# Loading and folding the Fourier input weights before the last modulation chunks

## The chip, the cores and the metric

The kernel runs on one core of a Trainium2 chip. The metric is the device time of one execution in microseconds (us), as the median of several runs. The core has five engines with instruction streams of their own: PE (TensorE, matrix multiply, with weight loads shown apart as PEld), DVE (VectorE), ACT (ScalarE), POOL (GpSimd) and SP (SyncE, which here only issues transfers). Sixteen DMA engines move the data. Each engine carries out its instructions in the order in which they were put into its queue.

## The reference

One encoder layer is applied to two sequences of 1024 tokens with 1024 channels, each with a conditioning vector `c`.

```python
mod = silu(c) @ w_ada + b_ada                  # 6 x 1024: shift, scale, gate, twice
h = rmsnorm(x, g_mix) * (1.0 + sc1) + sh1
z = h @ w_in                                   # q latent 256, kv latent 128, rotary key 64, Fourier 512
y_mla = mla_group(z[:, :256], z[:, 256:384], z[:, 384:448], ...)   # latent attention, 4 heads
y_four = fourier_group(z[:, 448:], w_four)     # real part of a 2-D FFT over tokens and 64 channels, 8 groups
x = x + ga1 * (concat([y_mla, y_four]) @ w_out)
h2 = rmsnorm(x, g_ffn) * (1.0 + sc2) + sh2
x = x + ga2 * ((silu(h2 @ w_gate) * (h2 @ w_up)) @ w_down)         # inner width 2816
y = rmsnorm(x, g_final)
```

All is float32. The change touches only how the weights of the Fourier part of `w_in` are made ready.

## The kernel before

Matrix products are made from two parts of each operand: `split` (lines 59 to 61) rounds a tile to a high part on ACT and takes the rest as a low part on DVE, and `mm3` (lines 70 to 73) multiplies high by high, high by low and low by high, so that lines 71, 72 and 73 carry nearly all matmuls. PSUM has eight banks, which are handed out in turn; a bank is free again when its readers are done.

The first stage reads `x` in eight pairs of 128-token blocks, four pairs for each sequence. A pair goes through these steps. `norm` (line 348) loads two blocks of `x`, squares them on ACT (L356), forms the reciprocal root on POOL (`rstd`, L95 to L102) and scales on DVE (L360). `flip` (line 363), four times per pair, transposes two of the eight channel chunks on PE (L374), applies the modulation on ACT (L377, tile `hf`) and splits the result into `hh` and `hl`. `zproj` (line 395), once for each block, multiplies by the 448 columns of the latents, `wz_h` and `wz_l`, then takes norms and the rotary key (L404 to L417), which gives `lat`. `latents` (line 425) transposes that (L431). `evenodd` (line 381) forms sum and difference of the pair's two blocks on POOL (L390) and splits them into `eoh` and `eol`, for which there are the buffers `eoh0`, `eol0`, `eoh1`, `eol1`. `fourier_in` (line 438) multiplies them by the Fourier input weights `wcs_h` and `wcs_l`. The function `pair` (line 507) sets these steps in order, with a step of `extras` (further weights, among them the folds of L242 and the second half of the modulation) between them.

Before the first pair stand the weights. `fold_q`, `fold_out` and `fold_pe` fold gains and small matrices into larger ones. The modulation vector is made from eight chunks of `w_ada`, 1 MB each: `mod_load` issues a chunk's transfer on SP, `mod_mm` (L207) multiplies it when it has landed, and after the last of them `mod_vecs` (L138 to L148) turns the row into the scales and shifts that every flip needs. The chunks share a few buffers (two `wada` buffers, and `hh0`, `hh1`, `hl1`, `hf`, which the pairs use later), so a load often has to wait until a chunk has been multiplied. `wz_load` and `wz_split` bring in the 448 latent columns in two halves, of four chunks each. `prep_wcs(i, wf)` (lines 330 to 346) folds the Fourier weights: for chunk `i` four matmuls of a slice of `wf` by the small matrix `c2` into one bank, then three casts on ACT (L337 twice, L342) and three subtractions on DVE (L338 twice, L343). Over the eight chunks these are 32 matmuls, which the profile counts as 64, 24 casts and 24 subtractions.

In the kernel before, `c2` and the Fourier weights `wfT` (two loads into the `wada` buffers, lines 489 to 493) are issued after the last modulation chunk, and the eight `prep_wcs` (lines 500 and 501) come after the flips of pair 0 and the norm of pair 1, ahead of its first `zproj`.

The order in each engine's queue is not simply that of the code. A planner walks the instructions with its own estimate of their costs: among those that it holds ready, the one that the code has first goes first, and ready work from later in the code can be put into a time in which it believes an engine idle. An instruction can be held back by hand: `behind()` (line 63) makes everything in its block go behind the last `split` on the engine concerned, ACT or DVE. It holds back no transfer and nothing on PE or POOL.

Of the kernel before, what the change touches and what calls it, by code (L numbers as in the profile page):

```python
# [12 lines left out]
F32 = mybir.dt.float32  # L13
# [8 lines left out]
P = 128  # L22
# [28 lines left out]
def hybrid_encoder_kernel(ctx: ExitStack, tc: tile.TileContext, a: dict):  # L51
    nc = tc.nc
# [3 lines left out]
    def rd(t):  # L56
        return t.bitcast(F32)

    def split(hi, lo, src):
        here["a"] = nc.scalar.copy(hi, src).ins  # L60
        here["v"] = nc.vector.tensor_tensor(out=lo, in0=src, in1=rd(hi), op=ALU.subtract).ins  # L61

    def behind():

        st = ExitStack()
        st.enter_context(tc.issue_after(here["a"]))
        st.enter_context(tc.issue_after(here["v"]))
        return st
# [63 lines left out]
    def rows(j, u):  # L132
        return slice(512 * u + P * j, 512 * u + P * j + P)
# [22 lines left out]
    with ExitStack() as st:  # L156
        p1b = st.enter_context(ExitStack())
        w2 = p1b.enter_context(tc.tile_pool(name="p1b", bufs=1, side="right", reuse_waits="tile"))
        w = st.enter_context(tc.tile_pool(name="p1", bufs=1, reuse_waits="tile"))
        pp = st.enter_context(tc.tile_pool(name="p1_ps", bufs=8, space=PSUM, reuse_waits="tile"))  # L160

        def bank():
            return pp.tile([P, 512], F32, tag="b", name="bank")

        def xtile():
            return w2.tile([P, D], F32, tag="x", name="xt", bufs=4)

        def stile(name):
            return w.tile([P, 512], F32, tag="sk", name=name, bufs=3)
# [9 lines left out]
        c2 = w.tile([P, P], F32, name="c2")  # L179
# [12 lines left out]
        def wada_tile():  # L192
            return w2.tile([P, 4, 512], F32, tag="wada", name="wada", bufs=2)

        def mod_load(c, cols, wt):
            for j, (lo_, n) in enumerate(cols):
                nj = n // 512
                nc.sync.dma_start(
                    wt[:, j * nj : (j + 1) * nj, :],
                    a["w_ada"][c * P : (c + 1) * P, lo_ : lo_ + n].rearrange("p (j n) -> p j n", n=512))  # L200
            return wt

        def mod_mm(key, c, wt):
            if c == 0:
                mods[key] = bank()
            for j in range(4):
                nc.tensor.matmul(  # L207
                    mods[key][32 * j : 32 * j + 32, :], scT[:, c, :], wt[:, j, :], start=(c == 0), stop=(c == NC - 1))

        def mod_row(key):  # L210
            mr = stile("modrow")
            nc.vector.tensor_copy(mr, mods.pop(key))
            return mr
# [24 lines left out]
        def fold_out(h, wo2, wuvT, gq):  # L238
            for g in range(2):
                gs = slice(512 * g, 512 * g + 512)  # L240
                ps = bank()
                nc.tensor.matmul(ps, wuvT[:, h, :], wo2[:, h % 2, gs], start=True, stop=True)  # L242
                so = stile("so")
                nc.vector.tensor_scalar(out=so, in0=ps, scalar1=gq[:, 2:3], scalar2=None, op0=ALU.mult)
                (nc.gpsimd if h < 2 else nc.sync).dma_start(wo_d[:, h, gs], so)
# [75 lines left out]
        def wz_load(i, t):  # L321
            t = t[:, : 4 * DZ].rearrange("p (a b) -> p a b", a=4)
            nc.sync.dma_start(t, a["wz"][:, i : i + 4, :])
            return t

        def wz_split(i, t):
            for b in range(0, 4, 2):
                split(wz_h[:, i + b : i + b + 2, :], wz_l[:, i + b : i + b + 2, :], t[:, b : b + 2, :])

        def prep_wcs(i, wf):  # L330
            ps = bank().rearrange("p (a b) -> p a b", a=4)
            for p in range(4):
                nc.tensor.matmul(ps[:, p, :], wf[:, p, (i % 4) * P : (i % 4 + 1) * P], c2, start=True, stop=True)
            for v, sl in ((ps[:, :, 0:64], slice(0, NCOS)), (ps[:, :, 64:128], slice(NZC, NCS))):
                h = wcs_h[:, i, sl].rearrange("p (a b) -> p a b", a=4)
                l = wcs_l[:, i, sl].rearrange("p (a b) -> p a b", a=4)
                nc.scalar.copy(h, v)  # L337
                nc.vector.tensor_tensor(out=l, in0=v, in1=rd(h), op=ALU.subtract)  # L338
            v = ps[:, :, 64:128:32].unsqueeze(1).broadcast_to([P, 3, 4, 2])
            h = wcs_h[:, i, NCOS:NZC].rearrange("p (k a b) -> p k a b", k=3, a=4)  # L340
            l = wcs_l[:, i, NCOS:NZC].rearrange("p (k a b) -> p k a b", k=3, a=4)
            nc.scalar.copy(h, v)  # L342
            nc.vector.tensor_tensor(out=l, in0=v, in1=rd(h), op=ALU.subtract)  # L343
# [4 lines left out]
        def norm(k):  # L348
            s, j = pairs[k]
            ms = tiny.tile([P, 2], F32, name="ms")  # L350
            xt = []
            for u in range(2):
                t = xtile()
                nc.sync.dma_start(t, xs[s][rows(j, u), :])
                jk = w.tile([P, D], BF16, tag="junk", name="junk", bufs=1)
                nc.scalar.activation(jk, t, AF.Square, scale=1.0 / 32.0, accum_out=ms[:, u : u + 1])  # L356
                xt.append(t)
            r = rstd(ms, 2)
            for u in range(2):
                nc.vector.tensor_scalar(out=xt[u], in0=xt[u], scalar1=r[:, u : u + 1], scalar2=None, op0=ALU.mult)  # L360
            st1["x", k] = xt

        def flip(k, g):
            s, j = pairs[k]
            if g == 0:
                st1["hf", k] = w2.tile([P, NC, 2, P], F32, tag="hf", name="hf", bufs=1)
                st1["hh", k] = w.tile([P, NC, 2, P], F32R, tag=f"hh{k % 2}", name="hh")
                st1["hl", k] = w.tile([P, NC, 2, P], F32R, tag=f"hl{k % 2}", name="hl")
            hf, xt = st1["hf", k], st1["x", k]
            pt = bank().rearrange("p (c u t) -> p c u t", c=2, u=2)  # L370
            for c in range(2):
                for u in range(2):
                    cc = 2 * g + c
                    nc.tensor.transpose(pt[:, c, u, :], xt[u][:, cc * P : (cc + 1) * P], ident)  # L374
            for c in range(2):
                cc = 2 * g + c
                nc.scalar.activation(hf[:, cc], pt[:, c], AF.Identity, bias=sh1[s][:, cc : cc + 1], scale=s1[s][:, cc : cc + 1])  # L377
            gs = slice(2 * g, 2 * g + 2)
            split(st1["hh", k][:, gs], st1["hl", k][:, gs], hf[:, gs])
# [74 lines left out]
        def wide(tag, shape=(P, 4, 512)):  # L454
            return (w2 if tag == "hf" else w).tile(list(shape), F32, tag=tag, name="wide")
# [12 lines left out]
        mod_mm(0, 0, wt[0])  # L468
        mod_mm(0, 1, wt[1])
        wt = [mod_load(2, cols0, wide("hh1")), mod_load(3, cols0, wada_tile())]  # L470
        fold_out(0, wo2, wuvT, gq)
        fold_out(1, wo2, wuvT, gq)
        fold_pe(wpe, gq)
        mod_mm(0, 2, wt[0])
        mod_mm(0, 3, wt[1])
        wt = [mod_load(4, cols0, wada_tile()), mod_load(5, cols0, wide("hh1"))]
        nc.sync.dma_start(bT, a["bT"])
        nc.sync.dma_start(gT, a["gT"])
# [2 lines left out]
        mod_mm(0, 4, wt[0])  # L481
        mod_mm(0, 5, wt[1])
        wt = [mod_load(6, cols0, wide("hh0")), mod_load(7, cols0, wada_tile())]
        wz_split(0, wz0)
        wz1 = wz_load(4, wide("hl1", (P, 4 * 512)))
        mod_mm(0, 6, wt[0])
        mod_mm(0, 7, wt[1])
        mod_vecs(mod_row(0), bank, bT, gT, 0, 0, s1, sh1)
        nc.sync.dma_start(c2, a["c2"])
        wf = []  # L490
        for q in range(2):
            wf.append(wada_tile())
            nc.sync.dma_start(wf[q], a["wfT"][:, :, 512 * q : 512 * q + 512])
        for g in range(4):
            flip(0, g)
        wz_split(4, wz1)
        norm(1)
        nc.sync.dma_start(ropec, a["ropec"])
        nc.sync.dma_start(ropes, a["ropes"])
        for i in range(8):  # L500
            prep_wcs(i, wf[i // 4])
        zproj(0, 0)
        evenodd(0)
        nk = len(pairs)
# [93 lines left out]
    with ExitStack() as st:  # L598
        early = st.enter_context(ExitStack())
        wa = early.enter_context(tc.tile_pool(name="p2a", bufs=1, reuse_waits="tile"))  # L600
        w = st.enter_context(tc.tile_pool(name="p2", bufs=1, side="right", reuse_waits="tile"))
# [235 lines left out]
    with ExitStack() as st:  # L837
        w = st.enter_context(tc.tile_pool(name="p3", bufs=1, side="right", reuse_waits="tile"))
# [144 lines left out]
        for k in range(nit + 4):  # L983
            if k >= nit:
                i = k - nit
# [3 lines left out]
            if k < nit:  # L989
# [3 lines left out]
                i = k % 8  # L993
# [21 lines left out]
    with ExitStack() as st:  # L1015
        w = st.enter_context(tc.tile_pool(name="p5", bufs=1, reuse_waits="tile"))
# [579 lines left out]
```

## Time and profile before

| | |
|---|---|
| median of three runs | 2137.72 us (lowest 2137.21) |
| profiled execution | 2136.0 us, span 2134.2 us |
| mean granted PE clock | 0.989 |
| busy: PE, DVE, ACT, POOL | 2054.9, 1420.7, 904.3, 826.7 us |
| moved by DMA | 371.11 MB, mean 174 GB/s |

The span is the time from the first to the last instruction that the profile shows. Busy time says how long an engine had something in work; PEclk is the share of its full clock that PE was granted. A row of a view in order of time gives the start, the duration, the engine, the line and operation, the tile written and the tiles read, the shape, the count, and in brackets the idle time of the engine ahead of it with what ended it.

### The profile page before, as it was taken

How to read it: one execution, taken by the hardware profiler on the slowest of the kernel's cores; microseconds unless marked ns; L12 is line 12 of the kernel's file. 1: busy time of each engine (PE TensorE's matmuls, PEld its weight loads, DVE VectorE, ACT ScalarE, POOL GpSimd, SP SyncE). 2: the span in 40 equal slices, each digit the busy share in tenths (PEclk: the TensorE clock that was granted, in tenths of full speed). 3: DMA queues.
4: the chain of work that ended last, by engine and by line, in shares of the span. 5: the costliest groups of instructions: out<-in, count | busy, mean ns of one | idle time of the engine just before them, and what ended most of it. 6: DMA issues, size and time to landing. Idle time of an engine off the chain costs nothing. (4 is left out here: it accounts for less than half of the span.)

```text
span 2134.2 us, 28930 instructions
## 1 busy us (share of the span) xinstructions
PE 2054.9 (96%) x10096; PEld 1671.4 (78%) x10096; DVE 1420.7 (67%) x2118; ACT 904.3 (42%) x1758; POOL 826.7 (39%) x1014
## 2 busy tenths in 40 slices
PE   5899998999999998999999999999999999999998
PEld 3787865888888886888888888887788888888876
DVE  2656655766676668786677667777866566557675
ACT  2655522555564546333333336444333333336441
POOL 1455202111222313797797720135545445420142
PEclk8999999999999999999999999999999999999999
DMA  9586656433545355564455468675423222248662
GB/s 366 189 248 181 225 189 234 102 92 92 138 119 124 119 182 203 187 212 168 159 206 188 153 227 290 226 237 175 148 79 119 99 101 97 99 135 290 230 226 101
DMA packets 184387, 371.11 MB, mean 174 GB/s; under 512 B 19280, under 2 KB 58832, under 8 KB 181168
## 3 DMA queue, kind: packets, MB, share of 16 engines
q1 hardware_dynamic: 166384, 313.80, 44.3%
q0 software_dynamic: 17856, 55.45, 8.8%
q8 instruction: 79, 1.29, 0.2%
q14 instruction: 68, 0.56, 0.1%
HBM read 257.18 MB, written 120.39 MB: 177 GB/s over the span
## 5 line engine op out<-in xcount | busy, mean ns | idle before, releaser
L71 PE MATMUL bank<-H,wh 128*128 128x512 f32 x1232 | 489.4, 397 | 13.5 <-DVE val L130 5.0
L73 PE MATMUL bank<-H,wl 128*128 128x512 f32 x1232 | 488.1, 396 | 1.5 <-DVE wl L61 1.5
L72 PE MATMUL bank<-H,wh 128*128 128x512 f32 x1232 | 488.2, 396 | 0.0
L130 DVE TENSOR_TENSOR val<-bank,val 128x512 f32<-128x512 f32 x244 | 167.0, 689 | 191.2 <-PE bank L73 183.4
L71 PEld LDWEIGHTS bank<-H,wh 128*128 128x128 f32 x1232 | 232.2, 188 | 73.2 <-DVE val L130 7.3
L73 PEld LDWEIGHTS bank<-H,wl 128*128 128x128 f32 x1232 | 232.0, 188 | 58.5 <-DVE wl L61 2.3
L72 PEld LDWEIGHTS bank<-H,wh 128*128 128x128 f32 x1232 | 232.0, 188 | 55.8
L61 DVE TENSOR_TENSOR wl<-draw,wh 128x512 fp32r<-128x512 f32 x286 | 200.9, 737 | 80.9 <-ACT wh L60 79.8
L60 ACT CAST wh<-draw 128x512 fp32r<-128x512 f32 x286 | 169.3, 619 | 155.3 <-PE bank L72 76.9
L72 PE MATMUL bank<-wl,wh 128*128 128x512 f32 x572 | 223.7, 391 | 2.2 <-DVE wl L61 2.2
L130 POOL TENSOR_TENSOR val<-val 128x512 f32<-128x512 f32 x58 | 82.8, 1434 | 363.5 <-DVE val L1380 188.6
L73 PE MATMUL bank<-wh,wl 128*128 128x512 f32 x572 | 222.6, 389 | 0.0
L71 PE MATMUL bank<-wh 128*128 128x512 f32 x572 | 222.6, 389 | 0.0
L60 ACT CAST wh<-rgu 128x512 fp32r<-128x512 f32 x172 | 106.7, 621 | 269.4 <-PE bank L72 211.5
L60 ACT CAST wh<-val 128x512 fp32r<-128x512 f32 x133 | 82.2, 621 | 277.6 <-PE bank L72 249.4
L61 DVE TENSOR_TENSOR wl<-val,wh 128x512 fp32r<-128x512 f32 x133 | 139.3, 1049 | 83.5 <-ACT wh L60 83.5
L61 DVE TENSOR_TENSOR wl<-rgu,wh 128x512 fp32r<-128x512 f32 x172 | 167.1, 972 | 4.8 <-ACT wh L60 4.2
L127 POOL TENSOR_TENSOR val<-rgu 128x512 f32<-128x512 f32 x84 | 122.0, 1452 | 120.3 <-DMA rgu<-in_wgu_dram 92.5
L72 PEld LDWEIGHTS bank<-wl,wh 128*128 128x128 f32 x572 | 107.3, 188 | 27.7 <-DVE wl L61 5.7
L71 PEld LDWEIGHTS bank<-wh 128*128 128x128 f32 x572 | 107.4, 188 | 22.3
L73 PEld LDWEIGHTS bank<-wh,wl 128*128 128x128 f32 x572 | 107.4, 188 | 22.1
L127 POOL TENSOR_TENSOR val<-val 128x512 f32<-128x512 f32 x89 | 119.4, 1358 | 1.3
(319 smaller groups left out, 4096.7 us busy)
## 6 DMA issues: line engine op xcount, KB each, us to landing
rgu<-in_wgu_dram SPq DMA_DIRECT2D x86, 512.0 KB, 4.2
draw<-s_d SPq DMA_DIRECT2D x143, 256.0 KB, 4.1
s_d<-val POOLq DMA_DIRECT2D x88, 256.0 KB, 4.1
draw<-t_d SPq DMA_DIRECT2D x88, 256.0 KB, 4.3
s_d<-val SPq DMA_DIRECT2D x66, 256.0 KB, 2.7
draw<-in_w_down_dram SPq DMA_DIRECT2D x55, 256.0 KB, 4.0
wada<-in_w_ada_dram SPq DMA_DIRECT2D x13, 1024.0 KB, 8.8
xt<-in_x_dram SPq DMA_DIRECT2D x16, 512.0 KB, 6.3
```

Source lines behind the costliest of these rows:

```text
L60: here["a"] = nc.scalar.copy(hi, src).ins
L61: here["v"] = nc.vector.tensor_tensor(out=lo, in0=src, in1=rd(hi), op=ALU.subtract).ins
L71: nc.tensor.matmul(out, lh, rh, start=first, stop=False, skip_group_check=cont)
L72: nc.tensor.matmul(out, lh, rl, start=False, stop=False, skip_group_check=cont)
L73: nc.tensor.matmul(out, ll, rh, start=False, stop=last, skip_group_check=cont)
L127: eng.tensor_tensor(out=out, in0=x, in1=y, op=ALU.subtract)
L130: eng.tensor_tensor(out=out, in0=x, in1=y, op=ALU.add)
```

## The change

The Fourier weights get four buffers of their own in place of two `wada` buffers: the bytes that `evenodd` later uses for the even and odd halves. Their loads and that of `c2` are issued behind chunk 3 of the modulation, ahead of chunks 4 to 7. The fold is done in two groups of four, one behind the multiplication of chunk 3, the other behind that of chunk 5. The second half of `wz` is loaded right behind chunk 7 as before, but its code stands ahead of the second group. Behind the modulation vectors, the split of the second half of `wz` is held behind the second flip's split, and the norm of pair 1 behind the fourth flip's.

```diff
         def prep_wcs(i, wf):
...
-                nc.tensor.matmul(ps[:, p, :], wf[:, p, (i % 4) * P : (i % 4 + 1) * P], c2, start=True, stop=True)
+                nc.tensor.matmul(ps[:, p, :], wf[:, p, (i % 2) * P : (i % 2 + 1) * P], c2, start=True, stop=True)
...
         wt = [mod_load(2, cols0, wide("hh1")), mod_load(3, cols0, wada_tile())]
+        nc.sync.dma_start(c2, a["c2"])
+        wf = []
+        for q in range(4):
+            wf.append(w.tile([P, 4, 256], F32, tag=("eoh0", "eol0", "eoh1", "eol1")[q], name="wf", bufs=1))
+            nc.sync.dma_start(wf[q], a["wfT"][:, :, 256 * q : 256 * q + 256])
         fold_out(0, wo2, wuvT, gq)
         fold_out(1, wo2, wuvT, gq)
         fold_pe(wpe, gq)
         mod_mm(0, 2, wt[0])
         mod_mm(0, 3, wt[1])
+        for i in range(4):
+            prep_wcs(i, wf[i // 2])
         wt = [mod_load(4, cols0, wada_tile()), mod_load(5, cols0, wide("hh1"))]
...
         mod_mm(0, 4, wt[0])
         mod_mm(0, 5, wt[1])
         wt = [mod_load(6, cols0, wide("hh0")), mod_load(7, cols0, wada_tile())]
+        wz1 = wz_load(4, wide("hl1", (P, 4 * 512)))
+        for i in range(4, 8):
+            prep_wcs(i, wf[i // 2])
+        wf.clear()
         wz_split(0, wz0)
-        wz1 = wz_load(4, wide("hl1", (P, 4 * 512)))
         mod_mm(0, 6, wt[0])
         mod_mm(0, 7, wt[1])
         mod_vecs(mod_row(0), bank, bT, gT, 0, 0, s1, sh1)
-        nc.sync.dma_start(c2, a["c2"])
-        wf = []
-        for q in range(2):
-            wf.append(wada_tile())
-            nc.sync.dma_start(wf[q], a["wfT"][:, :, 512 * q : 512 * q + 512])
-        for g in range(4):
-            flip(0, g)
-        wz_split(4, wz1)
-        norm(1)
+        flip(0, 0)
+        flip(0, 1)
+        with behind():
+            wz_split(4, wz1)
+        flip(0, 2)
+        flip(0, 3)
+        with behind():
+            norm(1)
         nc.sync.dma_start(ropec, a["ropec"])
         nc.sync.dma_start(ropes, a["ropes"])
-        for i in range(8):
-            prep_wcs(i, wf[i // 4])
         zproj(0, 0)
         evenodd(0)
```

## The prediction

> **What bounds the kernel now.** I read the engine totals first, then the stages of the span, because the edit lies wholly in the first fiftieth of it. In the stage table the columns after the window are its length, then busy time and count of PE, its weight loads, DVE, ACT and POOL, then PE's granted clock, the DMA share and GB/s.
>
> ```profile
> span 2134.2 us, 28930 instructions
> PE 2054.9 (96%) x10096; PEld 1671.4 (78%) x10096; DVE 1420.7 (67%) x2118; ACT 904.3 (42%) x1758; POOL 826.7 (39%) x1014
> ...
> 0.00:44.00 44.00, 22.39 (x88) 7.59 (x88) 10.33 (x21) 5.67 (x9) 6.47 (x20) 0.81 0.94 367
> 44.00:62.40 18.40, 16.08 (x109) 15.46 (x110) 12.84 (x37) 15.23 (x39) 4.35 (x8) 0.90 0.97 346
> 62.40:85.00 22.60, 18.31 (x102) 14.89 (x101) 17.32 (x48) 14.46 (x39) 10.87 (x20) 0.92 0.43 138
> 85.00:300.00 215.00, 210.50 (x1237) 164.69 (x1235) 130.56 (x262) 109.16 (x267) 80.47 (x174) 1.00 0.73 225
> 300.00:500.00 200.00, 189.05 (x1089) 155.60 (x1089) 135.91 (x275) 92.04 (x186) 32.02 (x48) 0.97 0.45 127
> 1100.00:1400.00 300.00, 300.00 (x1304) 244.39 (x1303) 207.55 (x264) 126.02 (x222) 129.49 (x119) 1.00 0.63 212
> ```
>
> PE is busy for 96% of the span and idle for 79.3 us. Of that, 21.6 us (44 - 22.39) lie in the first 44 us, 2.3 in the next stage and 4.3 in the third: 28 us is all that an edit of the start can reach. Later stages run with PE nearly full, 1100 to 1400 entirely so. Such a stage starts and ends earlier together with what precedes it, so a microsecond won before 85 us should arrive at the end, and one lost too.
>
> The first 44 us belong to the DMA. Two windows of that stage show it; below them are rows in order of time (start, duration, engine, line, what; in brackets the idle time before it and its releaser).
>
> ```profile
> 20.00:30.00 10.00, 4.96 (x29) 1.28 (x27) 2.25 (x3) 0.00 (x0) 2.30 (x5) 0.86 1.01 407
> 30.00:40.00 10.00, 2.76 (x12) 0.40 (x16) 2.05 (x3) 4.07 (x6) 1.74 (x6) 0.50 1.03 419
> ...
> 31.38 1.93 PE L207 MATMUL bank<-wide,scT 128*32 128x512 f32 x8 [5.34 <-DMA wide<-in_w_ada_dram]
> 39.18 1.94 PE L207 MATMUL bank<-wide,scT 128*32 128x512 f32 x8 [5.87 <-DMA wide<-in_w_ada_dram]
> 41.67 1.93 PE L207 MATMUL bank<-wada,scT 128*32 128x512 f32 x8 [0.56 <-DMA wada<-in_w_ada_dram]
> 44.51 1.09 PE L138 MATMUL bank<-ident,modrow 128*128 128x128 f32 x4 [0.91 <-DVE modrow L212]
> 45.39 3.01 PE L374 MATMUL bank<-ident,xt 128*128 128x128 f32 x16
> 48.24 7.31 PE L333 MATMUL bank<-c,wada 128*128 128x128 f32 x64
> 57.36 0.44 PE L71 MATMUL bank<-wz_h,hh 128*128 128x448 f32 x1 [1.81 <-DVE wcs_l L343]
> 62.39 1.03 PE L374 MATMUL bank<-ident,xt 128*128 128x128 f32 x8
> ```
>
> The 16 DMA engines are full (share 1.01 and 1.03) from 20 to 40 us, and the modulation chunks 5, 6 and 7 are multiplied when they land (31.4, 39.2, 41.7). From the end of chunk 7, at 43.60, the path is PE's own: transposes, the Fourier fold (L333, 7.31 us), 1.81 us for a bank that the fold's split still holds, and the first projection, 5.03 us, to 62.39.
>
> **The change part by part.**
>
> *Bytes moved ahead: +5.0 us.*
>
> ```profile
> wada<-in_wfT_dram SPq DMA_DIRECT2D x2, 1024.0 KB
> ```
>
> The Fourier weights, 2 x 1024 KB = 2.10 MB, were issued behind chunk 7, into its kind of buffer. Now they are ahead of chunk 4. At 419 GB/s they take 5.0 us, the DMA engines have nothing idle to put them in, so chunks 5 to 7 land 5.0 us later, chunk 7 near 46.7. Below, 4.5 is possible (the row at 407 GB/s leaves a little room); above, 5.9, if the second half of the fold, 32 matmuls, overruns the gap between chunks 5 and 6 at half clock. The four destinations are bytes that nothing has used yet, so SP has no new buffer to wait for; SP issues five loads where it issued three, at a place where DMA has megabytes queued, so the two more cost nothing there. SP's later issues, the second half of wz and x of pair 1, no longer stand behind a wait for chunk 7's buffer; the bytes before them are the same, so I count nothing for them either. POOL's queue is not passed.
>
> *The fold leaves the path: -9.1 us.* The 7.31 us of L333 and the 1.81 us behind them now lie in gaps where PE waits for chunks: the first half ahead of chunk 4, whose gap grows by the 5.0 us of new bytes, the second between chunks 5 and 6, where PE stood 5.87 us in the rows above. If that cover failed, the fold would cost its 7.31 again. Its splits go along:
>
> ```profile
> L337 ACT CAST wcs_h<-bank 128x256 fp32r<-128x256 f32 x16 | 5.3, 413 | 0.4 <-DVE wcs_l L338 0.3
> L338 DVE TENSOR_TENSOR wcs_l<-bank,wcs_h 128x256 fp32r<-128x256 f32 x16 | 6.1, 416 | 0.1
> L343 DVE TENSOR_TENSOR wcs_l<-bank,wcs_h 128x24 fp32r<-128x24 f32 x8 | 1.3, 176 | 0.2 <-ACT wcs_h L342 0.2
> ```
>
> About 7.4 us of DVE and somewhat less of ACT go where these were busy 10.33 and 5.67 us out of 44, so they are hidden.
>
> *Clock: -1.4 us.* PE's granted clock was 0.50 from 30 to 40, after long idle. With fold matmuls between the chunks PE should rest for no more than about a microsecond ahead of chunk 7, less than the 1.81 us behind which the projection still started at full speed.
>
> ```profile
> 22.85 1.04 PE L207 MATMUL bank<-wada,scT 128*32 128x512 f32 x8
> 68.13 0.60 PE L431 MATMUL bank<-ident,lat 128*128 128x128 f32 x4
> 69.44 1.88 PE L242 MATMUL bank<-wada,wuvT 128*128 128x512 f32 x4
> ```
>
> Chunk 7 then takes 1.04 in place of 1.93, and the four modulation transposes 0.60 in place of 1.09: -1.4. Bounds: nothing, and -2.3 when the flips' transposes gain as well.
>
> *The first projection is now paced by the flips: +2.8 us.* It used to find its input ready. Rows of ACT:
>
> ```profile
> 46.54 1.48 ACT L377 ACTIVATE hf<-bank,sh,s 128x256 f32<-128x256 f32 x3 [1.69 <-PE bank L374]
> 51.71 0.97 ACT L60 CAST wz_h<-wide 128x896 fp32r<-128x896 f32 x1
> 52.54 0.66 ACT L60 CAST hh<-hf 128x512 fp32r<-128x512 f32 x1
> 54.12 0.68 DVE L61 TENSOR_TENSOR hl<-hf,hh 128x512 fp32r<-128x512 f32 x1
> ```
>
> Four flips and one wz cast took 46.54 to 53.20; the other wz cast, once done ahead of them, is now behind flip 1 too: +0.9, so 54.1; the last low half adds 0.7: 54.8. Two of eight chunks are then left, six matmuls at 5.03/24 = 0.21: 56.1 on the old clock. Unpaced it would have been 62.39 - 9.1 = 53.3, hence +2.8. The bound below is 0, if the planner fills these gaps with the pair's second projection. The first projection so ends near 56.1 + 5.0 - 1.4 = 59.7.
>
> *Two stalls behind it: -5.0 us.*
>
> ```profile
> 66.88 0.68 DVE L61 TENSOR_TENSOR eol<-eo,eoh 128x512 fp32r<-128x512 f32 x1
> 72.58 0.40 PE L71 MATMUL bank<-wcs_h,eoh 128*128 128x280 f32 x1 [1.26 <-ACT hf L377]
> 78.34 0.48 DVE L416 TENSOR_SCALAR lat<-bank,rs_r 128x256 f32<-128x256 f32 x1 [1.67 <-POOL rs_r L102]
> 78.97 1.08 PE L431 MATMUL bank<-ident,lat 128*128 128x128 f32 x4 [3.03 <-DVE lat L416]
> 79.85 2.84 PE L242 MATMUL bank<-wada,wuvT 128*128 128x512 f32 x4
> 78.00:80.00 2.00, 1.03 (x5) 1.06 (x6) 1.66 (x5) 0.89 (x3) 0.77 (x4) 0.59 0.02 4
> ```
>
> DVE reached the even/odd halves' low parts only at 66.88, behind the fold's. POOL's second half, ACT's casts, and behind them the latent chain (ACT, POOL, DVE) were late in turn, and PE stood 1.26 + 3.03 us; the clock then fell to 0.59, and L431 and L242 took 1.4 us more than at full speed (1.08 - 0.60 and 2.84 - 1.88). Together 5.7. With the fold's 7.4 us gone from DVE I take 5.0; the rest is the idle per pair of the following stage, (215 - 210.5)/7 = 0.6, since the other seven pairs lie in it. Bounds: 0 and -5.7.
>
> *Pair 1's norm is put behind flip 3: +1.5 us.*
>
> ```profile
> 54.12 1.14 ACT L356 ACTIVATE junk<-xt 128x1024 bf16<-128x1024 f32 x1
> 57.01 0.23 POOL L95 TENSOR_SCALAR rs_v<-ms 128x2 f32<-128x2 f32 x1 [3.77 <-ACT wcs_h L342]
> 59.18 1.42 DVE L360 TENSOR_SCALAR xt<-xt,rs_r 128x1024 f32<-128x1024 f32 x2 [1.38 <-POOL rs_r L102]
> 72.24 0.48 DVE L259 TENSOR_TENSOR lw<-w 64x128 f32<-64x128 f32 x2
> ```
>
> From the last cast of flip 3 (54.1 + 5.0 - 1.4 = 57.7) two squares take 2.3, POOL's chain 2.2, DVE's scaling 1.4: 63.6. Pair 1's flips would ask PE for it at 59.7, and everything queued on PE behind them, the second projection first, would wait: 3.8 us, and 1.4 more if the clock falls. Against it: the planner moves ready work ahead, as it did with L259, which the code has several pairs later, and the second projection is 5 us of such work. Between 0 and 5.2 I take 1.5, by the 1.26 us that PE waited for a flip at 72.58.
>
> *The sum:* 5.0 - 9.1 - 1.4 + 2.8 - 5.0 + 1.5 = -6.2 us. The profiled execution took 2136.0 us, 1.8 outside its span; it becomes 2129.8. The median of the runs shown, 2137.72, lies 1.7 above it, so I forecast 2131.5. The planner orders the rest of the kernel anew; the idle 11 us of 300 to 500 show what an order can cost, and I allow 4 us either way.
>
> A rule that speaks against the edit: the Trainium skill, "TensorE: Matmul & The Clock Gate", Part 1 and Part 4, says that about 3.4 us of sustained work release the clock, and that transposes do not count as such work. By that rule the fold was the warm-up of the projection.
>
> ```profile
> 46.00:48.00 2.00, 2.00 (x13) 2.00 (x12) 1.80 (x10) 1.46 (x4) 0.00 (x0) 0.59 1.05 388
> ```
>
> Here the trace differs: only transposes ran from 44.51 to 48.13, and within this window the clock left 0.50.
>
> **The rivals.**
>
> *The projection starts cold.* The first 3 us of it run at half clock: 8 of 16 matmuls are done, 8 x 0.21 = +1.6, and the -1.4 is lost: 2134.5. For it: 27 to 47 us was at half clock. Against: the row just shown.
>
> *The latent chain still ends last.* The stalls at 72.58 and 78.97 stay, since POOL and ACT are in them as well as DVE: 5.0 - 9.1 - 1.4 + 2.8 + 1.5 = -1.2, so 2136.5. For it: 78.34 names POOL. Against: POOL was idle before, and stood behind late ACT work.
>
> *Slower: pair 1 arrives late.* The planner keeps the flips ahead of the second projection, PE waits 3.8 and pays 1.4 of clock, and as the chain hangs on the same engines the old stalls stay: 5.0 - 9.1 + 2.8 + 5.2 = +3.9, so 2141.6. It decides once this wait exceeds the stalls won by 1.3 us.
>
> *Everything is filled.* The second projection covers pacing and norm: 5.0 - 1.4 - 9.1 - 5.7 = -11.2, so 2126.5.
>
> *The change does not do what it says.* The planner leaves L333 behind chunk 7, or the loads behind the chunks: the path is that of before, 2137.7.
>
> **How the numbers follow.** Forecast 0.47, latent chain 0.20, slower 0.12, filled 0.10, cold 0.06, nothing done 0.05. With the 4 us of the planner around the outer cases the range is 2123 to 2142. Every case is within 2%, which is 43 us and about what a measurement of this kernel can tell from no change; I leave 0.02 and 0.03 for effects of the new order that no row here shows.
>
> **What would show it.** L333 in two groups before chunk 6, idle-free of DMA; chunk 7's L207 near 46.7 and shorter than 1.9; the first L71 at 448 columns near 53 with gaps, its group over by 60; no wait above 1 us at L431; L360 of pair 1 near 62 to 64. I would be wrong if chunk 7 came later than 48, if PE stood for L374 of pair 1, or if the idle time after 85 us changed by more than 4 us.

## The result and the profile after

The changed kernel takes 2142.09 us (median of 22 runs) against 2138.98 us for the kernel before beside it: a ratio of 1.0017, 95% interval 1.0012 to 1.0023. That is 3.1 us more by the medians, 3.6 by the ratio, well within the 2% and still clear of no change. The forecast was 2131.5, a gain of 6.2 us on the 2137.72 of before. The profiled execution took 2141.93 us.

The engine totals and the stage table of the changed kernel, columns as in the prediction:

```profile
span 2140.2 us, 28935 instructions
PE 2056.4 (96%) x10096; PEld 1674.6 (78%) x10096; DVE 1420.1 (66%) x2118; ACT 904.0 (42%) x1758; POOL 825.8 (39%) x1014
...
0.00:44.00 44.00, 25.39 (x136) 16.11 (x136) 13.61 (x40) 10.81 (x31) 6.08 (x18) 0.91 0.93 359
44.00:62.40 18.40, 11.71 (x58) 6.28 (x59) 12.21 (x25) 11.05 (x21) 3.05 (x4) 0.85 0.96 384
62.40:85.00 22.60, 16.39 (x85) 13.68 (x83) 13.19 (x37) 13.06 (x34) 13.04 (x28) 0.85 0.26 79
85.00:300.00 215.00, 210.34 (x1245) 165.89 (x1245) 129.66 (x262) 109.16 (x267) 79.72 (x173) 1.00 0.73 225
1100.00:1400.00 300.00, 300.00 (x1304) 244.81 (x1303) 206.85 (x261) 124.52 (x220) 129.78 (x120) 1.00 0.63 212
```

The fold is out of PE's path: the first stage holds 48 more of PE's instructions than before, the second 51 fewer. But the third, which should have become fuller, has 2 us less of PE work in it than before, at a mean clock of 0.85. PE's instructions in order of time show where:

```profile
26.83 10.01 PE L333 MATMUL bank<-c,wf 128*128 128x128 f32 x64 [2.60 <-DMA wf<-in_wfT_dram]
38.44 1.07 PE L207 MATMUL bank<-wide,scT 128*32 128x512 f32 x8 [0.60 <-DMA wide<-in_w_ada_dram]
45.79 1.93 PE L207 MATMUL bank<-wide,scT 128*32 128x512 f32 x8 [6.28 <-DMA wide<-in_w_ada_dram]
48.28 1.60 PE L207 MATMUL bank<-wada,scT 128*32 128x512 f32 x8 [0.56 <-DMA wada<-in_w_ada_dram]
50.80 0.63 PE L138 MATMUL bank<-ident,modrow 128*128 128x128 f32 x4 [0.92 <-DVE modrow L212]
51.26 1.91 PE L374 MATMUL bank<-ident,xt 128*128 128x128 f32 x16
54.45 0.47 PE L71 MATMUL bank<-wz_h,hh 128*128 128x448 f32 x1 [1.27 <-ACT hh L60]
58.98 0.47 PE L71 MATMUL bank<-wz_h,hh 128*128 128x448 f32 x1 [1.04 <-ACT hh L60]
62.73 0.36 PE L73 MATMUL bank<-wz_h,hl 128*128 128x448 f32 x1
69.30 0.66 PE L374 MATMUL bank<-ident,xt 128*128 128x128 f32 x2 [6.21 <-DVE xt L360]
76.96 0.60 PE L431 MATMUL bank<-ident,lat 128*128 128x128 f32 x4
```

The first four rows are the fold and chunks 5, 6 and 7; chunk 4 follows the fold at 36.77. The planner put all eight folds into one group ahead of chunk 4, and they run while the chunks arrive. Chunk 7 starts at 48.28 (41.67 before). The first projection is paced by the flips, as the prediction said, and ends at 63.09 (62.39 before). Then PE stands 6.21 us for pair 1's scaled `x`. No such wait was there before. And its clock (the third number from the right) falls:

```profile
64.00:66.00 2.00, 0.00 (x0) 0.00 (x0) 0.28 (x2) 0.88 (x2) 1.84 (x4) 1.00 0.01 4
66.00:68.00 2.00, 0.00 (x0) 0.00 (x0) 0.00 (x0) 0.36 (x1) 1.76 (x6) 0.62 0.00 0
68.00:70.00 2.00, 0.70 (x3) 0.73 (x4) 1.60 (x4) 0.00 (x0) 1.70 (x7) 0.50 0.00 0
70.00:72.00 2.00, 2.00 (x9) 1.76 (x9) 1.24 (x3) 0.24 (x1) 0.59 (x2) 0.50 0.04 8
```

What came between the flip and its input is in the rows of ACT, POOL and DVE, in the order of the chain:

```profile
60.28 1.10 ACT L356 ACTIVATE junk<-xt 128x1024 bf16<-128x1024 f32 x1
61.84 1.09 ACT L356 ACTIVATE junk<-xt 128x1024 bf16<-128x1024 f32 x1
62.78 1.27 POOL L390 TENSOR_TENSOR eo<-hf 128x512 f32<-128x512 f32 x1 [1.98 <-DVE eol L61]
64.14 0.23 POOL L95 TENSOR_SCALAR rs_v<-ms 128x2 f32<-128x2 f32 x1
64.45 1.26 POOL L390 TENSOR_TENSOR eo<-hf 128x512 f32<-128x512 f32 x1
65.67 0.72 POOL L98 TENSOR_TENSOR rs_y<-rs_v,mhalf 128x2 f32<-128x2 f32 x1
66.74 0.22 POOL L95 TENSOR_SCALAR rs_v<-mz 128x2 f32<-128x2 f32 x1
68.17 0.20 POOL L102 TENSOR_TENSOR rs_r<-rs_w,rs_y 128x2 f32<-128x2 f32 x1
68.40 1.42 DVE L360 TENSOR_SCALAR xt<-xt,rs_r 128x1024 f32<-128x1024 f32 x2 [4.12 <-POOL rs_r L102]
```

The squares, held behind flip 3, the last of the four, begin at 60.28. POOL is then busy with pair 0's sums and differences (L390), and mixes the first projection's root (`mz`) into pair 1's, which takes from 64.14 to 68.37; before it took 2.1 us (57.01 to 59.15).

A good mark for the end of the disturbed part is the copy of pair 0's second Fourier product, L446 writing `zs`, before and after:

```profile
85.57 0.37 ACT L446 COPY zs<-bank 128x256 f32<-128x256 f32 x1 [0.42 <-PE bank L73]
```

```profile
88.29 0.37 ACT L446 COPY zs<-bank 128x256 f32<-128x256 f32 x1 [2.23 <-PE bank L73]
```

2.7 us later at this mark, 3.1 later in the medians: the rest of the kernel adds nothing that the medians show. The two profiled spans are 6.0 us apart. The other 3.3 us lie behind the mark and are taken for the scatter of single executions; the idle time of PE after 85 us differs by only some 1 us.

### The profile page after: what moved, and what is told of

It reads as the page before. It is cut to its first block, busy times and chain, and to the rows that moved or that the text cites. A ratio compares the mean times of both kernels' runs of the same rounds, so it can differ in the third digit from the quotient of the medians.

```text
span 2140.2 us, 28935 instructions
## 1 busy us (share of the span) xinstructions
PE 2056.4 (96%) x10096; PEld 1674.6 (78%) x10096; DVE 1420.1 (66%) x2118; ACT 904.0 (42%) x1758; POOL 825.8 (39%) x1014
## 5 line engine op out<-in xcount | busy, mean ns | idle before, releaser
L71 PE MATMUL bank<-H,wh 128*128 128x512 f32 x1232 | 490.6, 398 | 11.5 <-DVE val L130 5.2
L71 PEld LDWEIGHTS bank<-H,wh 128*128 128x128 f32 x1232 | 233.0, 189 | 71.4 <-DVE val L130 7.8
L71 PE MATMUL bank<-wh 128*128 128x512 f32 x572 | 222.9, 390 | 0.3 <-ACT wh L60 0.3
L71 PEld LDWEIGHTS bank<-wh 128*128 128x128 f32 x572 | 107.4, 188 | 23.0 <-ACT wh L60 0.7
```

What stands on the lines that cost most here:

```text
L71: nc.tensor.matmul(out, lh, rh, start=first, stop=False, skip_group_check=cont)
```

## The experiments

Theory A: the fold on PE's path used to cover the norm of pair 1. With it gone, and the norm held back, PE waits for pair 1's `x` and then runs at half clock; that ate the gain. Theory B: the later modulation chunks alone make the loss. A ratio sets a kernel's runs against runs of the kernel before that were made beside them, so differences are taken from the ratios (0.001 is 2.1 us); differences of the plain medians can be a microsecond or two apart from these. The last two columns are from the single profiled execution: the mark, and the time from the start of chunk 7's product (L207) to it, which leaves the scatter of the loads out.

| kernel | median us | ratio to before, 95% interval | mark L446 `zs` | chunk 7 to mark |
|---|---|---|---|---|
| before | 2138.98 | 1 | 85.57 | 43.9 |
| the change | 2142.09 | 1.0017 (1.0012 to 1.0023) | 88.29 | 40.0 |
| no hold on the norm | 2138.89 | 0.9996 (0.9988 to 1.0005) | 86.10 | 37.5 |
| pair 1's flips later | 2140.03 | 0.9995 (0.9986 to 1.0004) | 85.86 | 36.0 |
| POOL: root first | 2144.13 | 1.0022 (1.0013 to 1.0032) | 89.68 | 40.7 |
| bytes ahead, fold late | 2148.93 | 1.0042 (1.0029 to 1.0054) | 94.39 | 47.1 |
| early fold, no holds | 2140.11 | 1.0006 (0.9997 to 1.0015) | 85.60 | 37.2 |
| rows of 2 KB | 2144.06 | 1.0027 (1.0015 to 1.0039) | 89.39 | 41.4 |
| both remedies | 2136.45 | 0.9993 (0.9984 to 1.0002) | 83.33 | 34.6 |
| both, rows of 2 KB | 2136.41 | 0.9987 (0.9978 to 0.9996) | 82.89 | 34.6 |

Median less mark is between 2052.8 and 2054.7 for all ten, although the marks differ by 11.5 us. So what happens before some 95 us decides, and by the medians it arrives at the end. In single executions that is hidden: from the mark to the end the ten profiled ones took between 2050.2 and 2057.4 us. The last column still holds one accident: in the change, and with pair 1's flips later, PE's clock was full again before pair 0's flips (1.91 us for 16 transposes), in the other six kernels with the early fold only in the course of them (2.80 to 3.48 us).

**No hold on the norm of pair 1.**

```diff
-        with behind():
-            norm(1)
+        norm(1)
```

> The changed kernel without the hold on the norm of pair 1 (the hold on the wz split stays). Theory A: the squares come earlier on ACT, the wait at pair 1's flip shrinks to under 3 us, and the flips of pair 0 lose up to 2.3 us to them: 1 to 4 us less than the changed kernel. Theory B: no gain, or up to 2 us more, since the first projection is paced by the flips.

Measured: 4.5 us less than the change (1.0017 to 0.9996), with the intervals apart. Its wait for pair 1's `x`, and DVE's scaling:

```profile
PE bank L374 <- DVE xt L360: 2.4, 1, 2.4
```

```profile
65.41 1.42 DVE L360 TENSOR_SCALAR xt<-xt,rs_r 128x1024 f32<-128x1024 f32 x2 [1.03 <-POOL rs_r L102]
```

The scaling comes 3.0 us earlier (68.40 in the change), the wait is 2.4 us in place of 6.2, and the time is that of the kernel before. But Theory A's reason, earlier squares, is the smaller part. The second square's readout ends at 63.14 here and at 63.02 in the change; against the first flip on ACT, which is 1.15 us later here, that is 1.0 us won. The rest is POOL's order: the planner now puts pair 1's root ahead of the last sums, and nothing is mixed into it.

```profile
63.23 0.23 POOL L95 TENSOR_SCALAR rs_v<-ms 128x2 f32<-128x2 f32 x1 [1.27 <-ACT junk L356]
65.17 0.20 POOL L102 TENSOR_TENSOR rs_r<-rs_w,rs_y 128x2 f32<-128x2 f32 x1
```

So the hold, with the order that the planner chooses under it, cost what the change lost.

**Pair 1's first flips behind the second projection.**

```diff
-            if k + 1 < nk:
+            if 0 < k < nk - 1:
                 flip(k + 1, 0)
                 flip(k + 1, 1)
             next(more, None)
             zproj(k, 1)
+            if k == 0:
+                flip(1, 0)
+                flip(1, 1)
```

> The changed kernel, with the first two flips of pair 1 put behind the second projection of pair 0 (only there). Theory A (PE's 6.2 us wait for pair 1's scaled x, and the half clock behind it, ate the gain): the 5 us of the second projection move ahead of that wait and also fill the pacing gaps of the first, so 3 to 6 us less than the changed kernel, that is 1 to 3 us less than the kernel before. Theory B (the later chunks alone make the loss: whatever PE does at this place, it ends at the same time, because pair 1's x comes late through ACT, POOL and DVE): within 1 us of the changed kernel.

```profile
56.31 0.47 PE L71 MATMUL bank<-wz_h,hh 128*128 128x448 f32 x1 [1.27 <-ACT hh L60]
71.20 0.41 PE L374 MATMUL bank<-ident,xt 128*128 128x128 f32 x2 [4.41 <-DVE xt L360]
```

Both projections run woven together from 56.31 to 66.79 (71.20 less 4.41), with no wait for a flip beyond the first. PE still stands 4.41 us for `x`, since that is as late as ever, but now the 5 us of the second projection are already done. The gain on the change is 4.7 us by the ratios (1.0017 to 0.9995) and 4.0 us in the profile, from chunk 7 to the mark: Theory A's 3 to 6. The plain medians show only 2.1. Chunk 7 itself started at 49.89 in this profile, 1.6 us later than in the change, from code that is the same up to there.

**Both remedies.** The two edits together.

> The changed kernel with both remedies: the first two flips of pair 1 behind the second projection, and no hold on the norm of pair 1. Theory A with two separate parts (x of pair 1 late, and PE's gaps while the flips pace the first projection): they add, 4 to 7 us less than the changed kernel, 1 to 4 less than the kernel before. Rival: one wait, which either remedy takes away; no less than the better of the two, some 3 us less than the changed kernel.

```profile
PE bank L374 <- DVE xt L360: 0.7, 2, 0.5
```

```profile
66.44 0.41 PE L374 MATMUL bank<-ident,xt 128*128 128x128 f32 x2 [0.52 <-DVE xt L360]
```

The wait is all but gone. From chunk 7 to the mark the two edits win 5.4 us over the change, where they won 2.6 and 4.0 alone: in the profile, two parts that overlap somewhat, the late norm and the gaps of the paced projection, which were filled once pair 1's flips no longer stood ahead in the code. The times do not confirm it. By the ratios the remedies win 4.5 and 4.7 us alone and 5.1 together, which is nearer to the rival, one wait that either takes away, and the three intervals overlap. Between the two readings the runs do not decide.

**POOL: pair 1's root ahead of pair 0's sums.**

```diff
         with behind():
             norm(1)
+        rs1 = here["p"]
...
         zproj(0, 0)
-        evenodd(0)
+        with tc.issue_after(rs1):
+            evenodd(0)
```

> The changed kernel, with pair 0's sums and differences on POOL held behind the reciprocal root of pair 1's norm. Theory A, and that POOL's order made half of the wait: the scaled x of pair 1 is there at 65 to 66 us in place of 69, the wait at its flip falls from 6.2 to about 3, the time by 3 to 5 us. Theory B: the scaled x comes as late, since the squares on ACT set it: within 1 us.

```profile
PE bank L374 <- DVE xt L360: 4.4, 1, 4.4
PE bank L431 <- DVE lat L416: 1.6, 1, 1.6
```

```profile
52.68 3.48 PE L374 MATMUL bank<-ident,xt 128*128 128x128 f32 x16
67.89 0.66 PE L374 MATMUL bank<-ident,xt 128*128 128x128 f32 x2 [4.42 <-DVE xt L360]
```

Theory A's 3 to 5 us did not come: 1.0022 with an interval that overlaps that of the change. The wait did fall, by 1.8 us, and the flip came 1.4 earlier. But a wait of 1.6 at the latents is new, and the first flips ran at half clock (3.48 us for 16 transposes, 1.91 in the change). POOL's order is a part of the wait; mended by itself it wins nothing. A part of what it won went again in DVE's scaling, which took 2.39 us in place of 1.42, while POOL's first late sum (L390) ran from 65.94 to 67.20:

```profile
66.02 2.39 DVE L360 TENSOR_SCALAR xt<-xt,rs_r 128x1024 f32<-128x1024 f32 x2 [3.78 <-POOL rs_r L102]
```

How much of the rest is the sums that are now late and how much the clock was not separated.

**The bytes ahead, the fold in its old place.** The loads of the change; flips, wz split, norm and fold in the order of the kernel before.

> The kernel before with the loads of the Fourier weights moved ahead as in the change, but the fold, the flips, the wz split and the norm in their old places. It prices the bytes by themselves. Theory A: chunk 7 is multiplied 5 to 6 us later and nothing else moves, so 5 to 6 us more than the kernel before; the early fold then has saved 2 to 3 us net of its stall. Theory B needs the same 3 us that the changed kernel lost, no more: the loss is the bytes alone.

```profile
47.29 1.94 PE L207 MATMUL bank<-wada,scT 128*32 128x512 f32 x8 [0.56 <-DMA wada<-in_w_ada_dram]
53.81 7.31 PE L333 MATMUL bank<-c,wf 128*128 128x128 f32 x64
65.14 0.71 PE L71 MATMUL bank<-wz_h,hh 128*128 128x448 f32 x1 [4.02 <-DVE wcs_l L343]
72.42 1.03 PE L374 MATMUL bank<-ident,xt 128*128 128x128 f32 x8
```

9.0 us more than the kernel before by the ratio, where 5 to 6 were expected. Chunk 7 is 5.6 later, as the bytes say. Then the wait for a bank is 4.02 in place of 1.81 (2.2 more), the clock falls in it, and the first projection takes 7.28 us in place of 5.03 (2.25 more): 10.0 at pair 1's flips. The longer wait stands in DVE's queue: pair 1's scaling (63.49 to 64.91) lies there behind only two of the fold's L338, where in the kernel before seven came ahead of it. So this kernel does not price the bytes quite by themselves. Theory B in its plain form falls: the early bytes without the early fold cost far more than the change lost, so the early fold does save, 5.3 us (1.0042 to 1.0017) in spite of the stall in the change.

**The early fold without any hold.** Flips, wz split and norm in the code's old order, loads and fold as in the change.

> The early loads and the early fold alone: flips, wz split and norm of pair 1 in the code's old order, without any hold. Theory A: as without the norm's hold, about 3 us less than the changed kernel, that is within 1 us of the kernel before. Rival (the hold of the wz split matters for the first projection): 1 us or more apart from the kernel without the norm's hold.

```profile
PE bank L374 <- DVE xt L360: 3.0, 1, 3.0
```

1.0006, 2.1 us above the kernel without the norm's hold, with intervals that overlap. The hold of the wz split is not told from no effect. The gain on the change is 2.4 us, not 3, and here the intervals overlap too: this second kernel without the norm's hold bears the first one out in direction, but weakly.

Beside the kernel with the early bytes and the late fold it gives the cleanest price of the fold's place, since the code of the two differs in nothing else: 1.0042 to 1.0006, 7.7 us, with the intervals far apart.

**Rows of 2 KB.** The first edit; `prep_wcs` then takes `wf[p // 2][:, p % 2, ...]`.

```diff
-            wf.append(w.tile([P, 4, 256], F32, tag=("eoh0", "eol0", "eoh1", "eol1")[q], name="wf", bufs=1))
-            nc.sync.dma_start(wf[q], a["wfT"][:, :, 256 * q : 256 * q + 256])
+            wf.append(w.tile([P, 2, 512], F32, tag=("eoh0", "eol0", "eoh1", "eol1")[q], name="wf", bufs=1))
+            nc.sync.dma_start(wf[q], a["wfT"][:, 2 * (q % 2) : 2 * (q % 2) + 2, 512 * (q // 2) : 512 * (q // 2) + 512])
```

> The changed kernel with the four loads of the Fourier weights cut another way: two of the four 128-row blocks by 512 columns each, so rows of 2 KB in place of 1 KB, the same bytes in the same place. Theory C (the chunks came later than the 5.0 us of bytes because the short rows slow the transfers: 404 against 415 GB/s from 8 to 40 us, 0.8 us): about 1 us less than the changed kernel, GB/s from 8 to 40 back near 415. Rival: the rest is scatter of the start; no change within 1 us.

> Both remedies and the 2 KB rows. If theory C holds, about 1 us less than with the remedies alone, and 2 to 5 us less than the kernel before; else the same as with the remedies alone.

The same stretch in the change, and then in this kernel:

```profile
8.00:40.00 32.00, 23.77 (x130) 14.75 (x130) 13.34 (x39) 6.48 (x25) 2.71 (x5) 0.89 1.03 404
```

```profile
8.00:40.00 32.00, 24.18 (x130) 13.07 (x130) 13.10 (x39) 6.62 (x25) 2.72 (x5) 1.00 1.03 412
```

The rate rose from 404 to 412 GB/s and chunk 7 started at 48.00 (48.28 in the change), but no time was won: 1.0027 against 1.0017, and 0.9987 against 0.9993 beside both remedies, each pair with intervals that overlap. The rate itself holds up: 404 to 407 GB/s in the seven kernels with early rows of 1 KB, 412 in both with 2 KB. But chunk 7 gained nothing when counted from chunk 0, which leaves out the scatter of the start: 36.4 us here (11.58 to 48.00), 35.5 in the change (12.74 to 48.28). Theory C's microsecond is not seen, and the runs are too few to exclude it. The wait for `x` was 6.2 us as in the change. Of the nine kernels, the one with both remedies and these rows is the only one whose interval lies below the kernel before.

## Why the prediction was wrong

It is followed here from mark to mark, change against before in the profiled executions.

- **The bytes, +5.0:** right in kind, too small. Chunk 7 started 6.6 us later. The kernels that load the weights ahead have it between 47.29 and 49.89, so 5.6 to 8.2 later; even chunk 0, ahead of every edit, started at 12.74 in the change and 11.57 before. Counted from chunk 0, the change has 35.5 us to chunk 7 and the kernel before 30.1, which is 5.4 more; the other 1.2 us came with the start. The upper bound of 5.9 left no room for that.
- **The fold, -9.1, and the pacing, +2.8:** right in the main, although the fold ran as one group and not as two. From the end of chunk 7 to the end of the first projection there were 18.8 us before (43.60 to 62.39) and are 13.2 now (49.88 to 63.09), -5.6; with the transposes' part of the clock the prediction had -6.8. The fold cost PE no wait of its own on the path.
- **The clock, -1.4:** it came in this profile (chunk 7 1.60 in place of 1.93, L138 0.63 in place of 1.09, the flips 1.91 in place of 3.01), but by luck. The reason given was that PE would rest no more than about a microsecond ahead of chunk 7. It stood 6.28 us ahead of chunk 6, which ran at half clock (1.93); the clock rose only in the course of chunk 7. In six of the eight kernels with the early fold chunk 7 took 1.93 or 1.94, L138 1.08 or 1.09 and the flips 2.80 to 3.48: no gain, or next to none.
- **The two old stalls, -5.0:** they went, as forecast. No wait at 72.58 or 78.97 has a counterpart, and from the latents (68.13 before, 76.96 after) to the mark the change gains 6.1 us: 8.8 behind at the first, 2.7 at the second. That they hang on the fold, the runs bear out: with the early bytes and the late fold they are there (0.95 and 2.62 us), with the early fold and no hold they are not. But PE's new wait also gave the latent chain time: in the kernel with both remedies, where PE hardly waits for `x`, it stands 1.40 and 0.79 us at the first latents.
- **Pair 1's norm, +1.5: the step that failed.** It measures 8.1 us: 6.21 of waiting, and 1.9 since the same transposes and second projection took 7.66 us (69.30 to 76.96) where they had taken 5.74 (62.39 to 68.13). The prediction had the scaled `x` at 63.6 and PE free at 59.7; they came at 69.8 and 63.1. Of the 6.2 us by which `x` was later, 2.6 are the squares' start (60.28 for 57.7, behind later chunks and a cast of the even half), 0.4 another such cast between the squares, 1.1 POOL's L390 ahead of the root (the last square's readout ends at 63.0, the root begins at 64.14), and 2.0 the work that POOL mixed into the root. POOL's queue was never looked at for what else the planner would put there: half of the lateness, 3.1 us, is POOL's. And the cover that was counted on, the second projection moved ahead, did not come: the planner left it behind the flips, and it moved only when the code was changed.

The sum, with the measured terms in the order bytes, chunk 7's clock, fold with pacing and the rest of the clock, norm, old stalls: 6.6 - 0.3 - 5.6 + 8.1 - 6.1 = +2.7, in place of -6.2. Two of the three signs of being wrong that the prediction named came: chunk 7 later than 48, and PE standing for L374 of pair 1. The upper end of its range was added up wrongly too: 4 us around its slowest case, 2141.6, gives 2145.6 and not 2142.

The slower rival, pair 1 arriving late, had the right place and the right sign at 2141.6, but for partly wrong reasons: its stall was priced at 5.2 in place of 8.1, and it kept the old stalls, which went. That its number is so near is luck, errors that cancel. The rival in which everything is filled was brought about with both remedies: their gain on the kernel before is 1.5 us, with the rows of 2 KB 2.8 (0.9993 and 0.9987), not 11. Later chunks are the smaller part of the difference: chunk 7 starts 7.1 us later than before there, where 5.0 were reckoned. The clock term did not come (chunk 7 1.93, L138 1.09), and not everything was filled: PE still waits 0.43 us for a flip, 0.7 for `x` and 2.2 at the latents. The clock was lost behind these waits, so that L242 took 3.33 us in place of 1.88. Together that is some 8 of the 9 us that are missing at the mark; the remainder was not traced.

The Trainium skill, "TensorE: Matmul & The Clock Gate", Part 1, says that the window in which activity is counted runs freely, about 3.4 us long, so that the point of a change depends on where in it the work falls. The transposes are in keeping with that, 1.91 and 3.48 us for the same 16 with the same work ahead of them, but no run here set the phase of that window apart. That transposes do not release the clock, as the Trainium skill has it in Part 4 of the same page, the prediction had weighed against a row of the kernel before; here too the rival of a cold first projection fell, for its L71 at 54.45 in the change and its neighbours took no more than 0.48 us, where 0.72 and 0.58 were seen at half clock behind the wait of 6.21.

## What to carry to other kernels

Work on the critical path also covers what runs beside it: when it is moved away, list every chain that used to finish under it, and work out each one's new end through the queues of all its engines, with what else stands in them. A planner that follows the code's order need not fill a new gap with work that the code has further on, as it did not here; look which instruction stands first in the queue of the engine that will be idle. When work is held back by hand, look too at what the planner then lets go ahead of it on engines that the hold does not concern, POOL here. And price a wait on PE of a few microseconds with the half clock behind it: here 6.2 us cost 8.1. Last, count a start's transfers from the first of them that the edit leaves alone: the start itself moved by 1.2 us between single executions.

## What the runs showed of the hardware

POOL's tiny steps of the root (L99 to L102) take 0.19 or 0.20 us, but two of them took 0.60 and 0.58 while DVE scaled `x` from 68.40 to 69.82, in the changed kernel:

```profile
68.32 0.19 POOL L100 TENSOR_TENSOR rs_w<-rs_w,rs_v 128x2 f32<-128x2 f32 x1
68.60 0.60 POOL L101 TENSOR_SCALAR rs_w<-rs_w 128x2 f32<-128x2 f32 x1
69.29 0.58 POOL L102 TENSOR_TENSOR rs_r<-rs_w,rs_y 128x2 f32<-128x2 f32 x1
```

Two further kernels show the same pair of steps at 0.60 and 0.58 beside DVE's scaling (pair 1's flips later, and rows of 2 KB). The other way round, the scaling took 2.39 us in place of 1.42 in the kernel with POOL's other order, where POOL's L390 had begun 0.08 us ahead of it. That one held up the other is read from the times alone; no run took it apart. The Trainium skill, "SBUF — State Buffer", "Who interferes with whom", says that VectorE's tensor-scalar can take the port pair that it shares with GpSimd for the whole instruction, and that the other then waits; these rows agree.

A gap on PE can cost the clock as well, but no length of the gap decides it alone. A wait of 2.36 us was enough in the kernel without the norm's hold, where PE stood from 63.95 to 66.31; the clock is the third number from the right:

```profile
64.00:66.00 2.00, 0.00 (x0) 0.00 (x0) 0.97 (x2) 0.80 (x5) 1.59 (x6) 0.79 0.01 4
66.00:68.00 2.00, 1.70 (x6) 1.49 (x7) 1.15 (x5) 0.00 (x0) 1.70 (x4) 0.50 0.03 8
```

But in the same kernel 48 matmuls of the fold behind a wait of 2.38 us took 5.60 us, at full clock, and with the bytes ahead and the fold late, four transposes behind 2.62 us took 0.63, at full clock too. Behind the 4.41 us of the kernel with pair 1's flips later the clock was still full from 71 to 72 us and fell only at 72, with PE at work since 71.20. And short waits close together can lose it: with both remedies, PE was busy for only 0.63 of the 2 us from 68 to 70, between waits of 1.40 and 0.79 us, and then ran at half:

```profile
72.00:74.00 2.00, 2.00 (x4) 0.89 (x4) 0.88 (x2) 0.77 (x2) 2.00 (x3) 0.50 0.51 74
```
